# Block products in the last up stage of the first feed-forward network

## The chip, the cores and the metric

The kernel runs on one core of a Trainium2 chip. The metric is device time in microseconds (us) of one execution. The engines have their own instruction queues and run side by side: TensorE (PE in the profile, with its weight loads as PEld), VectorE (DVE), ScalarE (ACT), GpSimd (POOL) and SyncE (SP), which here only issues loads. POOL computes nothing in this kernel either; its queue carries a set of transfers from DRAM to DRAM.

## The reference, cut to what matters

Two layers, each a token mixer followed by a gated feed-forward network with a three-tap convolution between its two projections:

```python
def conv_ffn(h, up_w, conv_w, conv_b, down_w):
    u = dwconv(h @ up_w, conv_w, conv_b)
    a, v = jnp.split(u, 2, axis=-1)
    return (jax.nn.silu(a) * v) @ down_w

for i in range(DEPTH):                    # DEPTH = 2
    ...                                   # mixer: SSD scan (i = 0), differential attention (i = 1)
    xp = xp + p_g2 * conv_ffn(modulate(xp, norm_ffn_g[i], p_sh2, p_sc2), *ffn_p)
    xs = xs + s_g2 * conv_ffn(modulate(xs, norm_ffn_g[i], s_sh2, s_sc2), *ffn_p)
```

The model width is 1024, the hidden width 2816 (so the up projection has 2 × 2816 outputs). There are 640 tokens, 512 latent (xs) and 128 context (xp). All numbers are fp32.

## The kernel before, in words

**Matmuls.** Activations lie transposed, 128 features to a tile and 640 tokens along it. An fp32 number is held as a high part and a remainder, and each product is made of three matmuls: high × high, high × remainder, remainder × high. So each weight tile that arrives from DRAM (`raw`) is cast twice before use: ScalarE writes the high part `whi`, VectorE the remainder `wlo` (`split_w`). There are four `raw` buffers, and a load into one waits until VectorE has made the remainder of the tile that was in it. SP issues all these loads in one queue. `nextw` fetches the next weight tile in the order of a list (`weight_units`), loads some tiles ahead and casts `ahead` tiles ahead.

**The feed-forward network** (`ffn`, once per layer, l = 0 and 1). The hidden width makes 22 pairs of up tiles, one tile for the gate half `a`, one for the value half `v`. After each pair an epilogue runs: three convolution taps, SiLU, product, and the split into `mh` and `ml` (the high part and the remainder that the down projection reads). The pairs go in three groups (SUB); after each group, with one pair of lead, eight down tiles (`po`) add that group's share to the residual stream `xr`. For l = 0 the groups are pairs 0 to 7, 8 to 14 and 15 to 21, so that with the lead the last up stage makes pairs 16 to 21.

**A standard pair** is two up tiles of 8 × 3 × (256 + 384 columns): 96 matmuls for the pair.

**A pair by block products** (class `Blocks`). The two up tiles of a pair, the two halves of the 1024 inputs and the two halves of the 640 tokens form a 2 × 2 by 2 × 2 block product, which is made with seven products in place of eight. Each product is 4 × 3 matmuls of 320 columns, 84 for the pair. It needs sums of blocks on both sides:
- of activations, `T1`, `T2`, `T4` for each of four tiles, made once by `sums()`, and `T3`, which `finish_sums()` writes over parts of the activations themselves (`h01h`, `h01l` in the first network);
- of weights, four per pair, made in DRAM by transfers that add into their target (`weight_sums`, tile `wsum`, on POOL's queue, each transfer 768 KB for three pairs). They begin with small marks that make the queue wait for a certain `mh`, and they are later loaded like other weights, in two halves of 256 KB for one `raw` tile.

Products are accumulated in PSUM banks `ba`, `bb` and `bc`; between them ScalarE copies a bank (into `ua` or `uv`) and VectorE adds another bank to that copy. Products 3 and 4 of a pair are made while the next pair is under way (`third`, `fourth`); those of the last pair come within the first two down tiles (`between`).

Before the change the second network (l = 1) makes its pairs 5 to 21 this way (`STD = 5`), and the first network none.

**What else runs beside.** During the first network VectorE also computes the second layer's modulation (`mod_rest`, tiles `mw`, `cbc` and `junk`), as a task that advances at each `hook` between matmuls. A task can be finished at once with `drain`. The order of instructions on each engine is fixed when the program is built, by a scheduler; the tables of rows below show that order.

Of the kernel before, what the change touches and what calls it, by code (L numbers as in the profile page):

```python
# [41 lines left out]
STD = 5  # L42
# [8 lines left out]
class Blocks:  # L51
# [4 lines left out]
    def __init__(self, st, h, epilogue, pool):  # L56
        self.st, self.h, self.epilogue, self.pool = st, h, epilogue, pool
        self.pend = None
        self.spare = None
        self.half = None  # L60

    def sums(self):
# [3 lines left out]
        place = ["p"] * 5 + ["s"] + ["f"] * 6  # L66
        c1, c2 = slice(0, HT), slice(HT, T)
        for j in range(4):
# [17 lines left out]
            for i, x in ((1, t1), (2, t2), (4, t4)):  # L86
                pl, nm = place.pop(), f"T{i}_{j}"
                t = (st.slot("f", nm, F32R, bufs=NF) if pl == "f" else st.slot("sq", nm, F32R, bufs=1) if pl == "s"
                     else st.slot("T", nm, F32R, bufs=5, pool=self.pool))
# [81 lines left out]
class Step:  # L171
# [516 lines left out]
    def ffn(self, l, h, nextnorm, pool):  # L688
# [28 lines left out]
        blk = None  # L717
# [7 lines left out]
        for s, (k0, k1) in enumerate(sub):  # L725
# [3 lines left out]
            while done < end:  # L729
                if l and done >= STD:  # L730
                    blk.pair(done)
                else:
# [3 lines left out]
                    if l and done == STD - 1:  # L736
                        self.drain(sums)
                        blk.finish_sums()
                done += 1
            self.down = True  # L740
            if last and self.modtask:
                self.drain(self.modtask)
            if s == 1 - l:
                half = 3 * SUMS
                ends = range(STD, STD + half, SUMS) if l == 0 else range(STD + half, FT, SUMS)
                for p in ends:
                    self.weight_sums(p, min(p + SUMS, FT), mid[done - 2][0].bitcast(F32)[0:1, 0:2])
            if not last:
                self.project_out(mid, range(k0, k1), self.gate(l, 1), after=blk and blk.between)
            else:  # L750
                self.project_last(mid, range(k0, k1), self.gate(l, 1), nextnorm, parts="CD" if l else "AB",
                                  after=blk and blk.between)
# [550 lines left out]
    def weight_units(self):  # L1303
# [10 lines left out]
        def ffn(l):  # L1314
            both = lambda t: [(a["w_blk"][t].rearrange("h p n -> p h n"), wide)] if l else [(a["w_up"][t], wide)]
# [3 lines left out]
            def piece(i, p):  # L1319
                if i in (1, 2, 4):  # L1320
                    return a["w_blk"][p + FT * (i == 4), int(i > 1)], 512
                return (lambda: self.wsum[p - STD, (5, 6, 7, 3).index(i)]), 512

# [185 lines left out]
```

## Time and profile before

| | us |
|---|---|
| runs, median of 3 | 1874.46 (1874.0 to 1875.87) |
| profiled execution | 1877.01 |
| its span, first to last instruction | 1875.2 |
| TensorE busy | 1839.6 (98%) |
| VectorE busy | 1429.4 (76%) |
| ScalarE busy | 983.9 (52%) |
| mean granted TensorE clock | 0.991 |

The first network's stages in the trace: first up stage from 593, first down 699 to 755, second up 755 to 853.6, second down 853.6 to 903.4, last up 903.4 to 988.0, last down to about 1040. Attention fills 1040 to 1409, the second network the rest.

How to read it: the page is one execution. A row of the groups gives the line, engine, operation, out<-in with the program's tile names without their numbers, the shape, the count, then busy time and mean ns of one, then the idle time of the engine ahead of it and what ended it. In a timeline row the bracket at the end says how long the engine stood before it and for what; no bracket means that it did not stand. Lines are those of the kernel before: 220 is ScalarE's helper, 226 and 223 VectorE's, 229 the matmul, 252 the weight load and 1364 the weight sums.

### The profile page before, as it was taken

The numbers are of one execution on the slowest core, as the hardware profiler recorded it, in microseconds if no ns is written. First come the engines' busy times: TensorE is split into PE (matmuls) and PEld (weight loads), VectorE is DVE, ScalarE is ACT, GpSimd is POOL, SyncE is SP. The second block draws the span as 40 slices with busy tenths as digits, with TensorE's granted clock in tenths as the row PEclk, the third lists the DMA queues.
The fourth block names the chain that finished last, engine by engine and source line by source line (L and its number), as shares of the span: only waits on it lengthen the run. The fifth ranks groups of instructions, "written<-read, shape, count | busy, mean of one in ns | idle before, by whom it ended". The sixth has DMA issues, their size and how long they took to land.

```text
span 1875.2 us, 33004 instructions
## 1 busy us (share of the span) xinstructions
PE 1839.6 (98%) x13129; PEld 1727.2 (92%) x13129; DVE 1429.4 (76%) x2759; ACT 983.9 (52%) x1825; POOL 41.7 (2%) x64
## 2 busy tenths in 40 slices
PE   7999999999999999999999999999999999999997
PEld 4799899989989999999999988888899999999996
DVE  4689999999848999984454878778779874874864
ACT  2479686879426441342343566566546543643641
POOL 0000000000000000001110000000000011100000
PEclk9999999999999999999999999999999999999998
DMA  9734334346543656546773212111032268953421
GB/s 342 249 116 140 100 122 134 113 131 174 183 148 102 192 180 214 194 131 198 212 195 93 88 38 65 57 44 54 22 118 68 87 182 235 258 160 102 141 79 57
DMA packets 98386, 258.76 MB, mean 138 GB/s; under 512 B 11468, under 2 KB 18232, under 8 KB 93752
## 3 DMA queue, kind: packets, MB, share of 16 engines
q1 hardware_dynamic: 92152, 220.47, 36.3%
q0 software_dynamic: 5504, 35.66, 8.2%
q8 instruction: 103, 1.69, 0.4%
q10 hardware_dynamic: 576, 0.52, 0.1%
q14 instruction: 51, 0.42, 0.1%
HBM read 250.65 MB, written 41.61 MB: 156 GB/s over the span
## 4 chain that ended last, share of the span: by engine, by line
PE 93%; DVE 3%; ACT 2%; DMA 1%; issue 1%; SPq 0%; DVEq 0%; ACTq 0%
PE po L229 26%; PE up L229 18%; PE z L229 6%; PE x L229 5%; PE bc L229 5%; PE ba L229 5%; PE st L229 5%; PE bb L229 5%; PE v L229 3%; PE yp L229 3%; PE q L229 2%; PE sl L229 2%; PE k L229 2%; PE ov L229 2%; PE in L229 1%; PE wt L1237 1%
## 5 line engine op out<-in xcount | busy, mean ns | idle before, releaser
L220 ACT ACTIVATE whi<-raw 128x1024 fp32r<-128x1024 f32 (+4 forms) x257 | 261.9, 1020 | 363.9 <-PE po L229 226.1
L226 DVE TENSOR_TENSOR wlo<-raw,whi 128x1024 fp32r<-128x1024 f32 (+4 forms) x257 | 301.3, 1173 | 102.7 <-ACT whi L220 91.2
L223 DVE SCALAR_TENSOR_TENSOR xr<-po,mod,xr 128x256 f32<-128x256 f32 (+2 forms) x231 | 88.9, 433 | 148.7 <-PE po L229 148.6
L229 PE MATMUL po<-ml,whi 128*128 128x256 f32 (+1 forms) x704 | 168.4, 310 | 0.0
L229 PE MATMUL po<-mh,whi 128*128 128x256 f32 (+1 forms) x704 | 168.2, 311 | 0.0
L229 PE MATMUL po<-mh,wlo 128*128 128x256 f32 (+1 forms) x704 | 168.0, 310 | 0.0
L229 PE MATMUL up<-h01h,wlo 128*128 128x256 f32 (+1 forms) x656 | 149.4, 308 | 0.0
L229 PE MATMUL up<-h01h,whi 128*128 128x256 f32 (+1 forms) x656 | 149.3, 308 | 0.0
L229 PE MATMUL up<-h01l,whi 128*128 128x256 f32 (+1 forms) x656 | 149.3, 308 | 0.0
L229 PEld LDWEIGHTS po<-mh,whi 128*128 128x128 f32 x704 | 128.5, 188 | 0.5 <-ACT mh L220 0.2
L229 PEld LDWEIGHTS po<-ml,whi 128*128 128x128 f32 x704 | 128.8, 188 | 0.1
L229 PEld LDWEIGHTS po<-mh,wlo 128*128 128x128 f32 x704 | 128.9, 188 | 0.0
L229 PEld LDWEIGHTS up<-h01h,wlo 128*128 128x128 f32 x656 | 119.3, 188 | 0.0
L229 PEld LDWEIGHTS up<-h01h,whi 128*128 128x128 f32 x656 | 119.3, 188 | 0.0
L229 PEld LDWEIGHTS up<-h01l,whi 128*128 128x128 f32 x656 | 119.2, 188 | 0.0
L220 ACT ACTIVATE mh<-cv 128x640 fp32r<-128x640 f32 x44 | 32.4, 737 | 81.9 <-DVE cv L226 81.9
L220 ACT ACTIVATE e<-sl,sm 128x640 f32<-128x640 f32 x64 | 50.3, 789 | 39.5 <-DVE sm L1174 39.1
L229 PE MATMUL z<-h00h,whi 128*128 128x256 f32 (+1 forms) x256 | 62.9, 325 | 0.0
L220 ACT ACTIVATE ca<-ca 128x640 f32<-128x640 f32 x44 | 32.4, 736 | 58.0 <-DVE ca L223 58.0
L220 ACT ACTIVATE e<-rb,Ctok 128x128 f32<-128x128 f32 x160 | 56.3, 389 | 11.6 <-issue 9.2
L229 PE MATMUL z<-h00l,whi 128*128 128x256 f32 (+1 forms) x256 | 59.8, 311 | 0.0
L229 PE MATMUL z<-h00h,wlo 128*128 128x256 f32 (+1 forms) x256 | 59.7, 312 | 0.0
(557 smaller groups left out, 5025.4 us busy)
## 6 DMA issues: line engine op xcount, KB each, us to landing
mw<-in_modT SPq DMA_DIRECT2D x48, 512.0 KB, 3.3
wsum<-in_w_blk POOLq DMA_DIRECT2D x30, 768.0 KB, 7.0
raw<-in_w_up SPq DMA_DIRECT2D x44, 512.0 KB, 4.3
raw<-in_w_in SPq DMA_DIRECT2D x40, 512.0 KB, 5.3
rb<-rowd SPq DMA_DIRECT2D x40, 512.0 KB, 5.1
raw<-wsum SPq DMA_DIRECT2D x68, 256.0 KB, 2.9
raw<-in_w_dn SPq DMA_DIRECT2D x32, 448.0 KB, 3.4
raw<-in_w_qkv SPq DMA_DIRECT2D x24, 512.0 KB, 3.4
```

Source lines behind the costliest of these rows:

```text
L220: return self.nc.scalar.activation(out, in_, func, **k)
L223: return self.nc.vector.scalar_tensor_tensor(out, in0, s, in1, op0, op1)
L226: return self.nc.vector.tensor_tensor(out, a, b, op)
L229: return self.nc.tensor.matmul(out, lhsT, rhs, start=start, stop=stop, **k)
L1237: nc.tensor.transpose(pm[:, b * P:(b + 1) * P], ws[b][:, kc * P:(kc + 1) * P], self.ident)
```

## The change

Pairs 16 to 21 of the first network, which are its last up stage, are made by block products too (`STD = (16, 5)`, one number for each network). For this:

- The activation sums of the first network are made as a task during its second down stage, and finished (`drain`, `finish_sums`) at that stage's end. Their tiles lie in buffers that are free then: six in `f`, one in `sq`, two in `mw`, three in `cbc`. `mod_rest`, which uses `mw` and `cbc`, is therefore drained after pair 15 instead of ahead of the last down stage.
- The weight sums of these six pairs are two groups of eight transfers and two marks each, put on POOL's queue after pair 12, waiting for `mh` of pair 11. They stand ahead of the second network's first three groups.
- All up weights of the first network are now read from the block layout that the second network used (`w_blk`, now for both), whose rows are two runs of 512 numbers in place of one of 1024.
- The outer taps of pairs 16 to 21 are negated, as block products give these tiles with the other sign.

```diff
-STD = 5
+STD = (16, 5)
...
+        std = STD[l]
...
+        place = [lambda n: self.slot("f", n, F32R, bufs=NF)] * 6 + [lambda n: self.slot("sq", n, F32R, bufs=1)]
         if l:
-            blk = Blocks(self, h, epilogue, pool)
-            t = cw[:, FT + STD:, 0:3]
-            nc.vector.tensor_scalar(t, t, -1.0, None, ALU.mult)
+            place += [lambda n: self.slot("T", n, F32R, bufs=5, pool=pool)] * 5
+        else:
+            place += [lambda n: self.slot("mw", n, F32R, D, 2, pool)[:, :T]] * 2 + [spare(j) for j in range(3)]
+        blk = Blocks(self, h, epilogue, place)
+        t = cw[:, FT + std:, 0:3]
+        nc.vector.tensor_scalar(t, t, -1.0, None, ALU.mult)
...
-                if l and done >= STD:
+                if done >= std:
                     blk.pair(done)
...
+                if l == 0 and done == 13:
+                    for p in range(std, FT, SUMS):
+                        self.weight_sums(0, p, min(p + SUMS, FT), mid[done - 2][0].bitcast(F32)[0:1, 0:2])
...
             self.down = True
-            if last and self.modtask:
-                self.drain(self.modtask)
...
+            if l == 0 and done == std:
+                self.drain(self.modtask)
+                sums = self.add(blk.sums(), 1)
+            after = blk.between if blk.pend else None
...
+            if l == 0 and done == std:
+                self.drain(sums)
+                blk.finish_sums()
...
         def ffn(l):
-            both = lambda t: [(a["w_blk"][t].rearrange("h p n -> p h n"), wide)] if l else [(a["w_up"][t], wide)]
+            both = lambda t: [(a["w_blk"][l, t].rearrange("h p n -> p h n"), wide)]
...
-                return (lambda: self.wsum[p - STD, (5, 6, 7, 3).index(i)]), 512
+                return (lambda: self.wsum[l][p - STD[l], (5, 6, 7, 3).index(i)]), 512
```

In the rows that follow, a number behind a name of a weight tile is its place in the list of weights (tiles 97 to 104 are the second down stage's), that behind `ua`, `uv`, `ca`, `cv`, `mh`, `ml` the pair, and the number after the underscore only tells instances apart.

ScalarE around the start of the last up stage (pair 16), before:

```order
L220 ACTIVATE whi105_10017<-raw105_9891 128x1024
L220 ACTIVATE whi106_10078<-raw106_9953 128x1024
L220 ACTIVATE whi107_10140<-raw107_10015 128x1024
L220 ACTIVATE whi108_10216<-raw108_10076 128x1024
L220 ACTIVATE whi109_10277<-raw109_10138 128x1024
L220 ACTIVATE whi110_10353<-raw110_10214 128x1024
L220 ACTIVATE uraw_10135<-up_10075 128x640
L220 ACTIVATE ca_10195<-uraw_10135,fcw0_6711 128x640
L220 ACTIVATE ca_10195<-ca_10195 128x640
L220 ACTIVATE whi111_10412<-raw111_10275 128x1024
```

and in the changed kernel:

```order
L217 ACTIVATE whi106_10191<-raw106_10086 128x1024
L217 ACTIVATE whi107_10216<-raw107_10139 128x1024
L217 ACTIVATE ua16_10205<-ba_10203 128x320
L217 ACTIVATE whi110_10284<-raw110_10213 128x1024
L217 ACTIVATE ua16_10205<-ba_10203 128x320
L217 ACTIVATE whi111_10321<-raw111_10250 128x1024
L217 ACTIVATE uv16_10206<-ba_10203 128x320
L217 ACTIVATE ua17_10303<-bb_10204 128x320
L217 ACTIVATE whi108_10220<-raw108_10207 128x1024
L217 ACTIVATE whi109_10252<-raw109_10210 128x1024
L217 ACTIVATE whi112_10354<-raw112_10281 128x1024
L217 ACTIVATE whi113_10405<-raw113_10318 128x1024
```

The casts of tiles 105 to 110 stood in a row, ahead of the first copy out of PSUM. Now the casts of 110 and 111 stand between copies of pair 16, and those of 108 and 109 come after a copy of pair 17 (`ua17`).

SP, the loads of the same weight tiles, before:

```order
L252 DMA raw105_9891<-in_w_up 128x1024
L252 DMA raw106_9953<-in_w_up 128x1024
L252 DMA raw107_10015<-in_w_up 128x1024
L252 DMA raw108_10076<-in_w_up 128x1024
L252 DMA raw109_10138<-in_w_up 128x1024
L252 DMA raw110_10214<-in_w_up 128x1024
```

and in the changed kernel:

```order
L249 DMA raw105_10034<-in_w_blk 128x2x512
L249 DMA raw106_10086<-wsum0_72 128x512 x2
L249 DMA raw107_10139<-wsum0_72 128x512
L249 DMA raw107_10139<-in_w_blk 128x512
L249 DMA raw108_10207<-in_w_blk 128x512
L249 DMA raw109_10210<-wsum0_72 128x512
L249 DMA raw109_10210<-in_w_blk 128x512
L249 DMA raw110_10213<-wsum0_72 128x512 x2
L249 DMA raw111_10250<-in_w_blk 128x2x512
L249 DMA raw112_10281<-wsum0_72 128x512
L249 DMA raw108_10207<-wsum0_72 128x512
L249 DMA raw112_10281<-wsum0_72 128x512
```

Each tile was one load of 1024 columns, in order. Now most consist of two halves, one of them or both from the sums, and the second half of tile 108 is issued behind the first half of tile 112.

VectorE, the remainder of weight tile 116, before (there it is the second tile of pair 21):

```order
L223 SCALAR_TENSOR_TENSOR cv_10473<-uraw_10465,fcw0_6711,cv_10473 128x511
L223 SCALAR_TENSOR_TENSOR cv_10473<-uraw_10465,fcw0_6711,cv_10473 128x127
L226 TENSOR_TENSOR cv_10473<-ca_10467,cv_10473 128x640
L226 TENSOR_TENSOR ml18_10482<-cv_10473,mh18_10481 128x640
L226 TENSOR_TENSOR wlo116_10755<-raw116_10620,whi116_10754 128x1024
L223 SCALAR_TENSOR_TENSOR ca_10601<-uraw_10542,fcw0_6711,ca_10601 128x511
L223 SCALAR_TENSOR_TENSOR ca_10601<-uraw_10542,fcw0_6711,ca_10601 128x127
```

and in the changed kernel (there it holds the weights of product 6 of pair 19 and of product 4 of pair 18):

```order
L223 TENSOR_TENSOR cv_10530<-ca_10524,cv_10530 128x640
L223 TENSOR_TENSOR uv18_10438<-uv18_10438,bb_10436 128x320
L223 TENSOR_TENSOR ml17_10539<-cv_10530,mh17_10538 128x640
L223 TENSOR_TENSOR ua19_10576<-ua19_10576,bc_10575 128x320
L223 TENSOR_TENSOR ua18_10437<-ua18_10437,bb_10436 128x320
L223 TENSOR_TENSOR wlo116_10508<-raw116_10439,whi116_10507 128x1024
L220 SCALAR_TENSOR_TENSOR ca_10657<-ua18_10437,fcw0_6712,ca_10657 128x511
L223 TENSOR_TENSOR wlo117_10558<-raw117_10472,whi117_10557 128x1024
L220 SCALAR_TENSOR_TENSOR ca_10657<-ua18_10437,fcw0_6712,ca_10657 128x511
```

Before, `wlo116` stood between the end of one pair's epilogue and the convolution of the next; now it stands directly behind an addition of a PSUM bank to `ua18`.

POOL's queue, first rows with transfers, before:

```order
L1367 DMA wsum_72<-mh14_9412 2x1x1 x5
L1364 DMA wsum_72<-in_w_blk 32x3x2048 x4
L1364 DMA wsum_72<-wsum_72 32x3x2048
L1364 DMA wsum_72<-in_w_blk 32x3x2048 x3
L1364 DMA wsum_72<-wsum_72 32x3x2048
L1364 DMA wsum_72<-in_w_blk 32x3x2048 x3
L1364 DMA wsum_72<-wsum_72 32x3x2048
L1367 DMA wsum_72<-mh14_9412 2x1x1
```

and in the changed kernel (`wsum0` belongs to the first network, `wsum1` to the second):

```order
L1385 DMA wsum0_72<-mh11_8999 2x1x1 x4
L1382 DMA wsum0_72<-in_w_blk 32x3x2048 x4
L1382 DMA wsum0_72<-wsum0_72 32x3x2048
L1382 DMA wsum0_72<-in_w_blk 32x3x2048 x3
L1382 DMA wsum0_72<-wsum0_72 32x3x2048
L1382 DMA wsum0_72<-in_w_blk 32x3x2048 x3
L1382 DMA wsum0_72<-wsum0_72 32x3x2048
L1385 DMA wsum1_73<-mh14_9434 2x1x1 x4
L1382 DMA wsum0_72<-in_w_blk 32x3x2048
L1382 DMA wsum1_73<-in_w_blk 32x3x2048
L1382 DMA wsum0_72<-wsum0_72 32x3x2048
L1382 DMA wsum1_73<-in_w_blk 32x3x2048
```

The queue began with the second network's sums, waiting for `mh14`. Now it begins with those of the first, waiting for `mh11`, and the second network's follow, partly mixed in.

More of the change, by code (lines that the diff above doesn't have):

```diff
@@ L1327, in ffn @@
                 end = min(k1 + 1, FT)
-                while done < end and not (l and done >= STD):
+                while done < min(end, STD[l]):
                     out += up(done)
@@ L1378, in run @@
         tc, nc, a = self.tc, self.nc, self.a
-        self.wsum = self.dram.tile([FT - STD, 4, P, 512], F32, tag="wsum", name="wsum")
+        self.wsum = [self.dram.tile([FT - STD[l], 4, P, 512], F32, tag=f"wsum{l}", name=f"wsum{l}") for l in range(2)]
         self.units = self.weight_units()
```

46 lines of the change are left out of this document (24 added, 22 removed).

## The prediction

> **What bounds the kernel now.** I read the page first, then busy times by stage, then the matmuls one by one where one stage ends and the next begins.
>
> ```profile
> PE 1839.6 (98%) x13129; PEld 1727.2 (92%) x13129; DVE 1429.4 (76%) x2759; ACT 983.9 (52%) x1825; POOL 41.7 (2%) x64
> PE 93%; DVE 3%; ACT 2%; DMA 1%; issue 1%; SPq 0%; DVEq 0%; ACTq 0%
> 790.00:818.00 28.00, 28.00 (x193) 28.00 (x192) 27.97 (x49) 13.02 (x16) 0.00 (x0) 1.00 0.54 174
> 818.00:848.00 30.00, 30.00 (x206) 30.00 (x206) 22.43 (x39) 15.07 (x19) 2.13 (x4) 1.00 0.27 81
> 855.00:900.00 45.00, 45.00 (x305) 45.00 (x305) 19.58 (x35) 8.86 (x10) 5.90 (x8) 1.00 0.77 213
> 900.00:990.00 90.00, 90.00 (x615) 90.00 (x614) 45.85 (x70) 39.18 (x48) 11.07 (x15) 1.00 0.78 198
> 1570.00:1656.00 86.00, 85.41 (x566) 82.78 (x565) 64.63 (x102) 50.75 (x73) 11.78 (x16) 1.00 0.88 241
> ```
>
> The columns of the stage rows are the stretch, its length, busy PE, PEld, DVE, ACT and POOL with counts, the granted clock, the DMA share and GB/s. TensorE is the bound: 98% of the span, 93% of the chain that ended last, and not a hundredth of a microsecond idle in the first network's stages, at a full granted clock. The second network, which already uses block products, does idle (85.41 of 86.00). So what the change removes from PE comes off the span one to one, and each wait it puts before a matmul goes on again.
>
> **The edit that saves: six pairs by seven products.**
>
> ```profile
> 903.44 0.46 PE L229 MATMUL up<-h01h,whi 128*128 128x256 f32 x2
> 903.73 0.46 PE L229 MATMUL up<-h01l,whi 128*128 128x256 f32 x2
> 987.97 0.45 PE L229 MATMUL po<-mh,whi 128*128 128x256 f32 x2
> 1485.23 0.31 PE L229 MATMUL ba<-h11h,wlo 128*128 128x320 f32 x1
> 1485.38 0.31 PE L229 MATMUL ba<-h11h,whi 128*128 128x320 f32 x1
> ```
>
> The last up stage runs from 903.44 to 987.97: 84.53 us for six pairs. A pair of matmuls (256 and 384 columns) takes 903.73 − 903.44 = 0.29 us; one block matmul of 320 columns takes 1485.38 − 1485.23 = 0.15. That is the same time per column, so the work follows the count: 84 of 320 columns in place of 96 (48 × 640/320). 84.53 × 12/96 = **10.57 us saved**. The two products that hang over (3 and 4 of pair 21) move into the first two down tiles and are in this count.
>
> [...]
>
> **What it costs: casts.** A standard tile needs one 1024-column cast (high half on ACT, remainder on DVE) for 48 matmuls; a block pair reads 3584 columns where a standard pair reads 2048, in less time. ACT has 39.18 of 90 us in that stage and DVE 45.85, so the sum fits, as it does in the second network (50.75 and 64.63 of 86). What matters is the order of the casts.
>
> ```profile
> L220 ACT ACTIVATE whi<-raw 128x1024 fp32r<-128x1024 f32 x30 | 31.7, 1058 | 54.1 <-PE po L229 26.0 <-PE bb L229 14.4 <-PE ba L229 11.2
> L226 DVE TENSOR_TENSOR wlo<-raw,whi 128x1024 fp32r<-128x1024 f32 x30 | 36.6, 1221 | 16.5 <-ACT whi L220 16.5
> L220 ACT ACTIVATE ua<-ba 128x320 f32<-128x320 f32 x12 | 5.1, 425 | 4.5 <-PE ba L229 4.5
> L226 DVE TENSOR_TENSOR ua<-ua,ba 128x320 f32<-128x320 f32 x6 | 2.9, 487 | 4.4 <-PE ba L229 4.4
> L229 PE MATMUL ba<-h11h,whi 128*128 128x320 f32 x71 | 22.7, 320 | 0.0
> 1493.67 0.56 PE L229 MATMUL ba<-T,whi 128*128 128x320 f32 x2 [0.53 <-ACT uv L220]
> 1636.69 0.41 PE L229 MATMUL bb<-h11h,whi 128*128 128x320 f32 x1 [0.59 <-ACT ua L220]
> PE bb L229 <- ACT ua L220: 1.3, 3, 0.6
> PE ba L229 <- ACT uv L220: 0.5, 1, 0.5
> ```
>
> Reading: a cast is 1.06 us on ACT and then 1.22 on DVE; a PSUM copy 0.42 on ACT, an add 0.49 on DVE; a matmul ends some 0.31 us after it begins, 0.16 after the next could begin. Where a copy must follow the very matmul before the waiting one, PE stood 0.53 to 0.59 us. All four waits of the second network's 17 pairs are of that kind, 1.8 us together; no cast is late there. In the changed order of the first network three casts stand late. I count matmuls from the first of pair 16.
>
> (a) Matmul 72, the first of product 2 of pair 17: ACT does the copy ua17, which needs matmul 71, and only then whi108, the tile of this product. PE stands 0.16 + 0.42 + 1.06 = 1.65 us with the handovers. After four matmuls (0.59) it needs wlo108, 1.25 behind whi108: another 0.66. Together **2.3**. Queued behind whi108 on ACT are whi109, whi112 and the first convolution of pair 16; those have over 20 matmuls of slack.
>
> (b) Matmul 264, the first of product 6 of pair 19: DVE's add ua18 needs matmul 263, 0.16 + 0.49 + handovers = 0.70, and wlo116 stands right behind it on DVE: 1.22 − 0.59 = 0.65. **1.35**.
>
> (c) Matmul 324 waits for the copy ua20 of matmul 323: **0.6**, like the quoted rows. Matmul 338 then waits for the add ua20 of 335 (0.4) and 340 for wlo119 behind it (0.9): **1.3**.
>
> (d) Seven further waits have 3 to 5 matmuls of slack (0.44 to 0.73 us) against a copy with handovers of 0.8 less what the last matmul overlaps. I take 0.2 for one with 3, and 0.4 for the one at matmul 101, where two adds on DVE follow the same matmul: **0.6**. Ends: 0, and 7 × 0.59 = 4.
>
> **Loads on SP.** The second half of raw108 is issued behind the first half of raw112, which waits for wlo110, whose whi110 stands behind the copy ua16. That is matmul 28 at 4.1 us, the add to 4.9, the cast to 6.1 after the stage's start. ACT wants raw108 at matmul 72 plus the copy, 11.2 us.
>
> ```profile
> raw<-wsum SPq DMA_DIRECT2D x28, 256.0 KB, 5.9
> raw<-in_w_blk SPq DMA_DIRECT2D x4, 512.0 KB, 5.4
> wsum<-in_w_blk POOLq DMA_DIRECT2D x18, 768.0 KB, 6.9
> raw<-in_w_up SPq DMA_DIRECT2D x12, 512.0 KB, 4.5
> ```
>
> The median landing of 256 KB beside the POOL queue's transfers is 5.9 us (the first two rows are of 1516 to 1656, the others of 840 to 990), so the half lands at 12.1: **0.9** more in (a). Ends 0 and 4, a landing near 9. The other loads of this network come from the block layout with shorter runs, 5.4 against 4.5 us; a tile has 7 us of PE time and loads run three tiles ahead, so they cost nothing; with that cover gone each would cost that 0.9.
>
> **The weight sums on POOL's queue.** Sixteen more transfers of 768 KB are made, from mh11 on.
>
> ```profile
> 805.97 0.74 ACT L220 ACTIVATE mh<-cv 128x640 fp32r<-128x640 f32 x1 [0.69 <-DVE cv L226]
> 845.87 2.77 POOL L1367 DMA_DIRECT2D wsum<-mh  x5 [845.42 <-ACT mh L220]
> 848.63 0.59 POOL L1364 DMA_DIRECT2D wsum<-in_w_blk  x1
> 864.62 0.90 POOL L1364 DMA_DIRECT2D wsum<-in_w_blk  x1 [6.88 <-issue]
> 874.21 0.59 POOL L1364 DMA_DIRECT2D wsum<-wsum  x1 [8.70 <-issue]
> 983.74 0.87 POOL L1364 DMA_DIRECT2D wsum<-in_w_blk  x1 [3.84 <-DMA wsum<-wsum]
> 1523.70 0.58 POOL L1364 DMA_DIRECT2D wsum<-in_w_blk  x1 [0.34 <-issue]
> 1654.64 0.84 POOL L1364 DMA_DIRECT2D wsum<-in_w_blk  x1 [4.74 <-DMA wsum<-wsum]
> ```
>
> Before, 24 such transfers are issued from 848.63 to 983.74: 5.87 us each. From mh11's end at 806.7, with small marks as before, the first goes at 810.5. The sum that raw106 reads, the seventh transfer, lands at 810.5 + 6 × 5.9 + 7 = 853; SP reaches raw106 only when wlo102 frees its buffer, about 879. The one for raw116 (the fourteenth) lands at 894 against 920. The last, for raw119 (two transfers of the second network's sums are mixed in, so the eighteenth), lands at 917; matmul 336 wants it at 903.4 + 49.4 + 5 = 958, less 7 for load and cast. At the traced pace all are in time: **0**. The second network's 24 then end near 1046 instead of 990, and are first read after 1482. DMA engines have room: 0.27 busy at 818 to 848, plus what these transfers added after (0.77 at 855 to 900).
>
> **The activation sums in the second down stage.**
>
> ```profile
> 854.53 1.09 DVE L226 TENSOR_TENSOR wlo<-raw,whi 128x896 fp32r<-128x896 f32 x1 [3.56 <-ACT whi L220]
> 866.29 1.13 DVE L223 SCALAR_TENSOR_TENSOR xr<-po,mod,xr 128x256 f32<-128x256 f32 x3 [3.74 <-PE po L229]
> 867.34 1.08 DVE L226 TENSOR_TENSOR wlo<-raw,whi 128x896 fp32r<-128x896 f32 x1
> 825.02 1.21 DVE L668 CUSTOM_DVE_ANT_0 junk<-mw,cbc 128x1024 bf16<-128x1024 f32 x1
> ```
>
> Four rounds of two 640-column adds, four 320-column sums and three remainders cost DVE 4 × (2 × 0.8 + 7 × 0.48) = 20 us, and 2 more for the rewritten halves; ACT 16 copies of 0.42, 7 us. DVE has 25.4 of 45 us free there. All rounds but the last come before wlo102: adding them up from wlo101 at 854.5, wlo102 ends near 879, and PE wants it at matmul −122, 885.5. Covered: **0**; with DVE 7 us later it would be a stall. The modulation that is drained earlier was done at 826, before that place: 0. Negating the taps is one small instruction in each network: 0.
>
> **Sum.** −10.57 + 2.3 + 0.9 + 1.35 + 0.6 + 1.3 + 0.6 = **−3.5 us**. Against the profiled span of 1875.2 that is 1871.7; that run took 1877.01 with what lies around it, and the median of the runs is 1874.46, so the median should be **1871.0**. A difference of 0.2% (3.75 us) is about what a measurement of this kernel tells from no change; the forecast lies almost on that bound.
>
> **Rivals.**
> 1. *The stalls don't come.* If casts and loads are only as late as in the second network, 1.8 us in 17 pairs becomes 0.7 in six: gain 9.9, 1864.6. For it: that network shows no late cast. Against: there at least 49 matmuls lie between a cast's last dependence and its use, here 0, 4 and 4. Chance 0.15.
> 2. *The weight sums come late, slower than before.* raw119 needs an average of under (951 − 7 − 810.5)/17 = 7.85 us per transfer; above it PE stands at matmul 336, with SP's queue behind it. At 8.7 us the eighteenth lands at 965, 14 us late: 1885. For it: one gap before was 874.21 − 864.62 = 9.6, and POOL's transfers now start while DVE is at 27.97 of 28 us. Against: in the second network, where DVE is 75% busy (64.63 of 86), 24 transfers from 1523.70 to 1654.64 take 5.7 us each, no longer than beside a DVE at 19.58 of 45. Chance 0.10. [...]
> 3. *The pinches are longer.* (d) at its upper end 4 and raw108 at 4: stalls of 13 instead of 7, 1877.5; a small loss. Chance 0.12.
> 4. *The change doesn't do what it says*: the saving is there but attention, whose loads and first casts are re-ordered, gives back 3 us: 1874. Its stages idled a few us in all before. Within the bound; chance 0.10.
>
> **How the numbers follow.** The forecast's own case, 1868 to 1873.5, has 0.53: some 0.30 of it below 1870.7 and 0.23 above. Faster: 0.30 + 0.15 = 0.45. Same: 0.23 + 0.10 + 0.03 of rival 3 = 0.36. Slower: 0.10 + 0.09 = 0.19. The range runs from rival 1 to rival 3, 1864.5 to 1878, and leaves out rival 2 and a little at each end.
>
> **What would show it.** The distance from the first block matmul to the first whole down tile; PE idle of 2 to 3.5 us named ACT whi, DVE wlo or a load some 10.6 us into the stage, about 1.4 at DVE ua or wlo near 42 us, and about 2 near 52 us; none in the down stage before it. POOL's issues should go from 810 on at 5.9 us. I would be wrong if PE waits there for raw<-wsum, if the three pinches are absent, or if the block matmuls step at other than 0.147 us.

## The result, and the profile after

The change made the kernel slower: 1883.95 us (median of 6 runs, 1882.19 to 1887.19) against 1874.1 (1872.26 to 1875.87) on the same chip, a ratio of 1.0056 [1.0044, 1.0069]. The forecast was 1871.0. The profiled execution took 1887.19 us with a span of 1885.4, 10.2 longer than the span before; it is the slowest of the six runs.

The page of the changed kernel, busy time by engine and the chain that ended last:

```profile
PE 1836.9 (97%) x13057; PEld 1719.3 (91%) x13057; DVE 1465.6 (78%) x2827; ACT 999.6 (53%) x1862; POOL 55.6 (3%) x84
...
PE 89%; DVE 4%; DMA 3%; ACT 2%; issue 1%; SPq 0%; DVEq 0%; ACTq 0%
```

PE has 72 matmuls fewer but only 2.7 us less busy time, and its share of the chain fell from 93% to 89%: it now waits. The waits of PE between 903 and 1110 us, from the first block product to the first scores of attention (engine, line, for whom; us in total, times, longest):

```profile
PE sl L226 <- ACT e L217: 2.8, 3, 1.6
PE ba L226 <- ACT uv L217: 2.7, 1, 2.7
PE bc L226 <- ACT whi L217: 1.8, 1, 1.8
PE q L226 <- ACT v L217: 1.6, 1, 1.6
PE bc L226 <- DVE wlo L223: 1.1, 2, 0.7
...
```

Before, PE waited only twice from 903 to 1110 us, 0.2 us at 1046.7 and 0.6 us at 1086.7. PE's timeline of the changed kernel has its waits one by one; the first row begins the block products, at the same time as the standard ones before (903.44):

```profile
903.38 0.30 PE L226 MATMUL ba<-h01h,whi 128*128 128x320 f32 x1
...
914.12 0.42 PE L226 MATMUL bb<-h01h,whi 128*128 128x320 f32 x1 [1.05 <-DVE uv L223]
917.94 0.41 PE L226 MATMUL bc<-h01h,whi 128*128 128x320 f32 x1 [1.79 <-ACT whi L217]
919.20 0.63 PE L226 MATMUL bc<-h01h,wlo 128*128 128x320 f32 x1 [0.41 <-DVE wlo L223]
919.63 0.47 PE L226 MATMUL bc<-h01h,whi 128*128 128x320 f32 x1
919.90 0.47 PE L226 MATMUL bc<-h01l,whi 128*128 128x320 f32 x1
...
922.76 0.31 PE L226 MATMUL bb<-h01h,whi 128*128 128x320 f32 x1
922.91 0.31 PE L226 MATMUL bb<-h01l,whi 128*128 128x320 f32 x1
...
949.99 0.53 PE L226 MATMUL bb<-T,whi 128*128 128x320 f32 x2 [0.67 <-DVE ua L223]
951.03 0.42 PE L226 MATMUL bb<-T,wlo 128*128 128x320 f32 x1 [0.23 <-DVE wlo L223]
960.03 0.42 PE L226 MATMUL ba<-h01h,whi 128*128 128x320 f32 x1 [0.53 <-ACT ua L217]
962.71 0.56 PE L226 MATMUL ba<-T,whi 128*128 128x320 f32 x2 [0.36 <-DVE ua L223]
963.94 0.41 PE L226 MATMUL bc<-h01h,wlo 128*128 128x320 f32 x1 [0.66 <-DVE wlo L223]
976.84 0.82 PE L226 MATMUL ba<-T,whi 128*128 128x320 f32 x2 [2.68 <-ACT uv L217]
```

The nine waits in brackets add up to 8.38 us. Behind the first three, matmuls step 919.90 − 919.63 = 0.27 us, not the 0.15 of 922.91 − 922.76. The stage rows show why: the granted clock (third last column).

```profile
919.00:923.00 4.00, 3.80 (x16) 3.80 (x17) 2.90 (x4) 0.78 (x1) 0.00 (x0) 0.58 0.96 206
923.00:975.00 52.00, 48.63 (x318) 46.31 (x316) 38.60 (x60) 29.38 (x41) 5.84 (x8) 1.00 0.86 243
975.00:979.00 4.00, 2.16 (x8) 2.16 (x9) 2.18 (x4) 2.01 (x3) 0.87 (x1) 0.74 1.00 340
979.00:983.00 4.00, 4.00 (x22) 3.73 (x22) 1.95 (x4) 1.83 (x3) 0.00 (x0) 0.83 1.01 224
```

After the first waits, and again after the single one of 2.68, the clock is lower for some 3 us. In shorter stretches the trace has 1.00 from 918.5 to 918.9 and 0.50 from 919.2 to 922.0, so the clock had already fallen when the third wait ended. Adding up, over all starts in the stage, by how much each step exceeds 0.147 (0.293 for a pair) gives 7.26 us, about 3 of it in these two slow stretches; most of the rest is at matmuls that wait for a copy, an add or a cast, and at the one behind each of them: these step 0.1 to 0.16 us longer, even where little or no idle time is recorded.

No trace here gives a rule for what makes the clock fall: here it fell after waits of 1.05 and 1.79 us, and after one of 2.68 (0.50 from 977.0 to 980.0); in e5 (below), behind waits of 1.05, 2.34 and 0.40 us at the same matmuls, the steps are 0.15 us again from the second matmul on, and not 0.27.

From the first block product to the last down matmul (1044.3 us) it is 140.9 us; before it was 136.0 (903.44 to 1039.4). So the change lost 4.9 there: −10.57, +8.38 and +7.26 make +5.1. From there to the first score matmul (`sl`) it is 40.2 us (1084.5), before 34.3: another 5.9.

### The profile page after: what moved, and what is told of

Same layout as the page of the kernel before. It is cut to its first block, busy times and chain, and to the rows that moved or that the text cites. A ratio compares the mean times of both kernels' runs of the same rounds, so it can differ in the third digit from the quotient of the medians.

```text
span 1885.4 us, 33063 instructions
## 1 busy us (share of the span) xinstructions
PE 1836.9 (97%) x13057; PEld 1719.3 (91%) x13057; DVE 1465.6 (78%) x2827; ACT 999.6 (53%) x1862; POOL 55.6 (3%) x84
## 4 chain that ended last, share of the span: by engine, by line
PE 89%; DVE 4%; DMA 3%; ACT 2%; issue 1%; SPq 0%; DVEq 0%; ACTq 0%
PE po L226 24%; PE up L226 13%; PE bb L226 6%; PE z L226 6%; PE ba L226 6%; PE x L226 5%; PE bc L226 5%; PE st L226 5%; PE v L226 3%; PE yp L226 3%; PE sl L226 2%; PE k L226 2%; PE q L226 2%; PE ov L226 2%; PE in L226 1%; PE wt L1255 1%
## 5 line engine op out<-in xcount | busy, mean ns | idle before, releaser
L217 ACT ACTIVATE whi<-raw 128x1024 fp32r<-128x1024 f32 (+4 forms) x266 | 270.4, 1020 | 326.6 <-PE po L226 199.2
L223 DVE TENSOR_TENSOR wlo<-raw,whi 128x1024 fp32r<-128x1024 f32 (+4 forms) x266 | 312.4, 1177 | 78.7 <-ACT whi L217 67.8
L226 PEld LDWEIGHTS po<-mh,whi 128*128 128x128 f32 x704 | 128.0, 188 | 1.0 <-ACT mh L217 0.8
L226 PE MATMUL up<-h01h,whi 128*128 128x256 f32 x464 | 105.6, 308 | 0.0
L226 PE MATMUL up<-h01h,wlo 128*128 128x256 f32 x464 | 105.6, 308 | 0.0
L226 PE MATMUL up<-h01l,whi 128*128 128x256 f32 x464 | 105.6, 308 | 0.0
L226 PEld LDWEIGHTS up<-h01h,whi 128*128 128x128 f32 x464 | 84.4, 188 | 0.0
L226 PEld LDWEIGHTS up<-h01l,whi 128*128 128x128 f32 x464 | 84.4, 188 | 0.0
L226 PEld LDWEIGHTS up<-h01h,wlo 128*128 128x128 f32 x464 | 84.4, 188 | 0.0
L226 PE MATMUL bb<-T,whi 128*128 128x320 f32 x264 | 61.4, 312 | 0.7 <-DVE ua L223 0.7
L665 DVE CUSTOM_DVE_ANT_0 junk<-mw,cbc 128x1024 bf16<-128x1024 f32 x48 | 58.6, 1221 | 3.5 <-DMA mw<-in_modT 3.5
```

The lines of the kernel that those rows point to most:

```text
L217: return self.nc.scalar.activation(out, in_, func, **k)
L223: return self.nc.vector.tensor_tensor(out, a, b, op)
L226: return self.nc.tensor.matmul(out, lhsT, rhs, start=start, stop=stop, **k)
L665: nc.vector.tensor_tensor_reduce(w if c else junk, w, cb[:, c, :], 1.0, 0.0, ALU.mult, ALU.add, self.mod[l][:, t, c:c + 1])
```

## The experiments

Three theories stood at the start, and all are about what the forecast costed at nothing or small. *Order*: the scheduler lists the casts and the loads as if the sums came late, and PE waits for what stands late in the list. *Crowding*: the sixteen transfers on POOL's queue take DMA time from loads at a place where something is short. *Attention*: the rope table's load, which now stands behind ten weight loads in SP's order and not six, delays attention. All edits are to the changed kernel unless said otherwise; medians with the range, the ratio to the kernel before in the same session with its 95% interval.

| run | median us (range, runs) | before | ratio |
|---|---|---|---|
| e1 sums after pair 8 | 1879.38 (1874.75–1882.63, 10) | 1874.13 | 1.0024 [1.0013, 1.0035] |
| e2 the same, rope early | 1879.17 (1874.67–1881.66, 6) | 1874.13 | 1.0028 [1.0016, 1.0039] |
| e3 second network's sums moved | 1907.49 (1905.38–1911.84, 4) | 1874.13 | 1.0186 [1.0171, 1.0201] |
| e4 before, rope late | 1875.14 (1872.07–1876.7, 11) | 1874.13 | 1.0006 [0.9997, 1.0015] |
| e5 changed, rope early | 1884.37 (1881.53–1889.52, 6) | 1874.23 | 1.0063 [1.0049, 1.0077] |
| e6 e5, sums after pair 11 | 1874.28 (1868.98–1881.38, 12) | 1874.23 | 1.0000 [0.9989, 1.0012] |
| e7 e5, sums after pair 10 | 1872.89 (1869.03–1877.36, 12) | 1874.23 | 0.9991 [0.9981, 1.0000] |
| e8 no sums for the first network | 1867.68 (1866.96–1869.91, 5) | 1874.23 | 0.9968 [0.9956, 0.9980] |
| e9 sums in the mixer | 1867.79 (1862.39–1870.95, 7) | 1873.4 | 0.9959 [0.9945, 0.9974] |
| e10 e9, transfers repeated, unread | 1872.06 (1867.59–1877.08, 11) | 1873.4 | 0.9994 [0.9983, 1.0004] |
| e11 changed again | 1883.11 (1879.54–1886.52, 6) | 1873.4 | 1.0048 [1.0033, 1.0063] |

**e1, the sums early.**

```diff
-                if l == 0 and done == 13:
+                if l == 0 and done == 9:
```

> The changed kernel with one edit: the first network's weight sums go on POOL's queue after pair 8 (waiting for mh7) instead of after pair 12. In the order that the scheduler then writes, the casts of tiles 108, 116 and 119 stand in front of the copies that they stood behind. Theory A (late casts in the order): the waits of 1.05, 1.8+0.4, 0.7+0.2 and 0.5+0.4+0.7 us in the last up stage shrink to at most 2 us in all, the two stretches of slow clock go, and the last down stage ends 6 us or more sooner than in the changed kernel (from 1044.3 to 1038 or less); the rope table stays behind eight loads of the query, key and value weights, so attention's start still loses some 5 us; total 1875 to 1878. Theory B (transfers crowd each other): the sums of the second network still run through the stage, loads still land after 6 us, and at least 5 us of waits stay; total 1881 or more.

The block stage was mended: one wait of 0.4 us is left, and from the first block product to the last down matmul it is 128.2 us. But the transfers now ran beside the modulation loads of the second up stage, and the first block product begins at 917.1, 13.7 us later than in the changed kernel. The total, 1879.4, lies between the two theories, each of which has a part. The stage's row, before and then in e1:

```profile
699.00:800.00 101.00, 101.00 (x690) 101.00 (x690) 99.21 (x177) 29.98 (x35) 0.00 (x0) 1.00 0.63 200
```

```profile
699.00:800.00 101.00, 93.37 (x621) 92.14 (x619) 76.40 (x135) 16.72 (x20) 9.73 (x13) 0.98 0.92 272
```

e1's issues in that stage (count, KB each, median us to landing), and its waits of PE and of DVE from 690 to 860 us:

```profile
mw<-in_modT SPq DMA_DIRECT2D x20, 512.0 KB, 7.1
wsum<-in_w_blk POOLq DMA_DIRECT2D x9, 768.0 KB, 9.6
```

```profile
PE up L226 <- ACT uraw L217: 5.8, 2, 4.8
PE up L226 <- DVE xr L220: 4.0, 2, 3.0
```

```profile
DVE junk L665 <- DMA mw<-in_modT: 24.8, 10, 3.6
```

DVE had 1.8 us to spare there before (99.21 of 101). The modulation loads land in 7.1 us and not 3.3, DVE waits 24.8 us for them, and PE waits 9.8 for DVE's and ACT's work behind that. So crowding is real, and of the places tried for these sums it cost most here, where DVE is full and fed by loads.

**e2 and e4, the rope table.** e2 is e1 with the first attention weight tile (number 134) cast outside the first network's pool, so that attention's small loads come earlier; e4 does the reverse to the kernel before (tile 125 cast inside the pool).

```diff
-            wp, t, b = (self.pw, "w", 3) if self.px is None or u % 5 < 3 else (self.px, "x", 2)
+            wp, t, b = (self.pw, "w", 3) if self.px is None or u % 5 < 3 or u == 134 else (self.px, "x", 2)
```

```diff
-            wp, t, b = (self.pw, "w", 3) if self.px is None or u % 5 < 3 else (self.px, "x", 2)
+            wp, t, b = (self.pw, "w", 3) if self.px is None or u % 5 < 3 and u != 125 else (self.px, "x", 2)
```

> As the run before, and the cast of weight tile 134 (the first tile of attention's projections) is put in the buffers that outlive the first network, instead of in the network's own pool; in the order the rope table's load then stands behind five weight loads, not eight. Theory A': the rope table waits for the network's memory, which tile 134 holds until attention's first tiles are done; with the tile elsewhere the load is issued near 1035 to 1045, PE reaches the first score matmul about 10 us after the first q matmul as before (it took 14 in the changed kernel), and 4 to 6 us come off against the run with the early sums alone: 1869 to 1873. Rival: attention starts late because of the POOL transfers that run until 1060; then nothing moves against that run.

> The kernel before with one edit: the cast of the first tile of attention's projections (125 there) is put in the first network's pool, as its number happens to do in the changed kernel. The up and down stages keep their order, the rope table's load moves from behind six weight loads to behind eight. Theory A': the load is issued near 1066 instead of 1039.8 and the kernel is 4 to 6 us slower, 1878 to 1880, all of it between 1040 and 1110. Rival (order of these loads does not matter, the crowded transfers do): no difference from before within 1 us.

In e2 the rope load went out at 1045.0 and not 1065.7 (e1), with no effect on the time (1869 to 1873 was expected, so the rival held); e1's stretch into attention was no longer than before. e2 loses in the second up stage as e1 does (PE waits 9.0 us from 690 to 860), though its lists on ACT, DVE and SP are row for row those of e10 (below), which has no wait of PE there; so that loss is made by the transfers, not by the order. In e4 it went out at 1061.5 and not 1039.8; the stretch grew from 34.3 to 35.9 us and the time by 0.06%, within what can be told. So a rope load some 20 us later, behind eight weight loads, is worth at most 1 to 2 us. The changed kernel has ten ahead of it, which e4 doesn't test.

**e3, the second network's sums moved into attention.**

```diff
-                for p in ends:
-                    self.weight_sums(1, p, min(p + SUMS, FT), mid[done - 2][0].bitcast(F32)[0:1, 0:2])
+        for p in range(STD[1], FT, SUMS):
+            self.weight_sums(1, p, min(p + SUMS, FT), self.cv[0:1, 0:2])
```

> The changed kernel with all weight sums of the second network made during attention (waiting for the table cv), so that the last up stage has only the end of the first network's own sums beside it; the casts of the last up stage stay in the changed kernel's order. Theory A: loads land in 3 to 4 us after the first 15 us, the wait of 2.7 us at the copy uv20 (ACT held by a cast whose down weights had not come) goes with the slow clock behind it, but the waits at matmuls 60, 72, 264, 324 and 338 stay, 5 to 6 us; the last down stage ends 4 to 5 us sooner; the rope table is still late, behind eight loads; total 1878 to 1880. Theory B: all waits of the stage vanish, 1872 or less.

The largest waits in the block stage:

```profile
PE bc L226 <- ACT whi L217: 1.5, 1, 1.5
PE bc L226 <- DVE wlo L223: 1.1, 2, 0.7
PE bb L226 <- DVE uv L223: 1.0, 1, 1.0
PE bb L226 <- DVE ua L223: 0.7, 1, 0.7
PE ba L226 <- ACT ua L217: 0.5, 1, 0.5
```

The block stage kept its pinches (5.4 us; the wait of 2.68 is gone), which therefore don't come from these transfers. That was theory A, but its total, 1878 to 1880, was missed by some 28 us, because attention lost far more. One kind of its small transfers between 1060 and 1300 us (in the kernel before it landed in 1.5 us), and its largest wait of PE, which the kernel before doesn't have:

```profile
out_kout<-kp SPq DMA_DIRECT2D x7, 64.0 KB, 5.8
```

```profile
PE wt L1250 <- ACT wpT L217: 11.2, 4, 3.5
```

**e5, e6 and e7, the sums one step at a time.** e5 is the changed kernel with e2's line and with all marks of a group of sums issued ahead of its transfers; e6 and e7 then start the first network's sums one and two pairs earlier.

```diff
-                    for p in range(std, FT, SUMS):
-                        self.weight_sums(0, p, min(p + SUMS, FT), mid[done - 2][0].bitcast(F32)[0:1, 0:2])
+                    ps = range(std, FT, SUMS)
+                    self.weight_marks(0, ps, mid[done - 2][0].bitcast(F32)[0:1, 0:2])
+                    for p in ps:
+                        self.weight_sums(0, p, min(p + SUMS, FT))
```

```diff
-                if l == 0 and done == 13:
+                if l == 0 and done == 12:
```

> The changed kernel with its sums at their old place and two edits that touch attention's start alone: the cast of weight tile 134 goes to the buffers that outlive the first network, and all marks of a set of weight sums are issued ahead of its transfers, so that no mark that reads the first network's mh stands late in POOL's queue. In the order the rope table's load then stands behind five weight loads, not ten. Theory: the 5.7 us that the changed kernel lost between its last down tile and its first score matmul come back (34 us for that stretch, not 40), the last up stage keeps its 5 to 8 us of waits; total 1877 to 1879. Rival (attention's start is slow because POOL's transfers run until 1060): the stretch stays at 40 us and the total at 1883.

> As the run before, and the first network's weight sums start one pair sooner, after pair 11 (waiting for mh10, about 792). In the order the casts of tiles 108 and 116 then stand in time; only the waits near matmuls 324 to 340 are left. Theory (late casts): the stage's waits fall from 8.4 us to 2 to 3 with no slow clock, the last down stage ends near 1034 to 1036, total 1866 to 1871. Rival (crowding): the transfers overlap the modulation's loads from 792 to 816, the second up stage loses what the last one gains; total 1874 or more.

> As the run before, one pair sooner still (after pair 10, waiting for mh9, about 777). Theory: the order of the last up stage is about the same as with pair 11, so its waits are too (2 to 3 us), and the only difference is the overlap with the modulation's loads until 816: 40 us instead of 24. If crowding grows with the overlap, the second up stage loses 1 to 4 us and the kernel is that much slower than with pair 11; with a start after pair 8 (110 us of overlap) it lost some 14 us.

e5 issued the rope load at 1042.5; in its trace, which is of its fastest execution, the stretch into attention is 36.4 us and not 40.2. The median didn't follow: it is as slow as the changed kernel, so this theory failed by its own number. One pair earlier (e6) is worth 10 us at once. The waits in the block stage, the four largest of e5 and then the three largest of e6:

```profile
PE bc L226 <- ACT whi L217: 2.3, 1, 2.3
PE ba L226 <- ACT uv L217: 1.7, 1, 1.7
PE bb L226 <- DVE uv L223: 1.2, 2, 1.1
PE bc L226 <- DVE wlo L223: 1.1, 2, 0.7
```

```profile
PE ba L226 <- DVE ua L223: 0.7, 1, 0.7
PE bc L226 <- DVE wlo L223: 0.6, 1, 0.6
PE ba L226 <- ACT ua L217: 0.5, 1, 0.5
```

As many transfers run in e6; the list of casts is another, and the largest waits are gone. e6's traced execution (1870.77) is in the range of its theory, but its median, 1874.28, is the rival's, though the second up stage loses nothing in the trace (the first block product is at 902.4). e7 has one wait of 2.3 us for `uv` again; that it is faster than e6, and not slower as expected, is within what can be told.

**e8, no sums for the first network.**

```diff
-                if l == 0 and done == 13:
-                    for p in range(std, FT, SUMS):
-                        self.weight_sums(0, p, min(p + SUMS, FT), mid[done - 2][0].bitcast(F32)[0:1, 0:2])
...
+                if l == 0:
+                    return a["w_blk"][l, p + FT * (i == 7), int(i == 6)], 512
```

> As the runs before, and no weight sums are made for the first network: products that need one read a plain block of the same weight in its place, loaded in the same two halves, so these six pairs' results are left out of what the kernel computes. All other work stays. This is what the block products are worth alone. Theory: 10.6 us saved, about 2.5 lost to short waits and restarts in the stage, none in the second up stage: total 1865 to 1867. If loads or casts still make PE stand for over 3 us here, the sums were not the cause of it.

So the block products by themselves, with their casts well placed and without their own sixteen transfers, are worth 6.5 us in the medians (1874.23 − 1867.68), not 10.57. The stage with its down tiles takes 128.0 us against 136.0.

**e9, the sums in the mixer.** e5 with the same sums issued some 310 us earlier (the lines after pair 12 go), where the mixer's output projection leaves the DMA engines free (from 495 to 620 us their share was 0.38; with the sums it is 0.78, and PE has no wait there). The lists of PE, ACT and DVE are e8's, row for row.

```diff
         hy = [self.split(xf[2 + i // 4][i % 4], f"y{8 + i}") for i in range(8)]
+        ps = range(STD[0], FT, SUMS)
+        self.weight_marks(0, ps, hy[0][0].bitcast(F32)[0:1, 0:2])
+        for p in ps:
+            self.weight_sums(0, p, min(p + SUMS, FT))
```

> The kernel of the rope experiment (tile 134 and the marks moved), and the first network's weight sums are made some 300 us sooner, beside the end of the mixer (waiting for y8, about 495), ahead of the modulation's loads. In the order all casts of the last up stage then stand in time, as without sums. Theory: what the changed kernel lost is the place of these transfers, by the order they bring and by the loads they crowd; here both are gone, so the total is that of the kernel without sums, 1866 to 1869, with under 1 us of waits in the last up stage and none in the second. Rival: the transfers cost what they cost wherever they run; then PE waits in the mixer between 500 and 600 and the total is 1872 or more.

It beats both kernels: 0.9959. The six pairs' block products pay when their weight sums are made out of the way. The last up stage itself is no emptier than in the changed kernel, since the second network's transfers now run there (DMA share 0.89 from 905 to 985 us, against 0.86). Nor is the mixer's place always free: in the trace of e10, which has the same program there, ACT waits 4.1 us for a load and PE then 2.2 us, near 550.

**e10 and e11, the crowd without the order.** e10 is e9 with the sixteen transfers made a second time, after pair 12, into a table that nobody reads; nothing on PE, ACT, DVE or SP is listed otherwise than in e9. e11 is the changed kernel again.

```diff
+                if l == 0 and done == 13:
+                    ps = range(std, FT, SUMS)
+                    self.weight_marks(2, ps, mid[done - 2][0].bitcast(F32)[0:1, 0:2])
+                    for p in ps:
+                        self.weight_sums(2, p, min(p + SUMS, FT))
```

> As the run before, and the same sixteen transfers are made a second time, after pair 12 as in the changed kernel, into a table that nobody reads. The order of every other engine is that of the run before, so this adds crowding alone, with the second network's sums pushed back as in the changed kernel. Theory A (order): with casts in time, late landings are covered; within 1.5 us of the run before. Theory B (crowding): loads land after 6 us and more, ACT and PE wait for some of them in the last up stage and the last down stage, differently in each execution: 4 to 8 us slower than the run before, and a spread of runs of 6 us or more where the run before has 3. What is left up to the 1884 of the rope experiment is then the order's.

> The changed kernel itself once more, beside the two runs before, for a second trace and more times. If the loss between the last down tile and the first score matmul is made by the place of the rope table's load in SP's queue, the stretch is 40 us in this trace too; if it comes from the state of POOL's transfers it can be anything from 34 to 40. The waits that the order makes (near matmuls 60, 72, 264, 324, 338) must be the same within 0.3 us; the one at the copy uv20, made by a late load, need not be. Total 1882 to 1886.

The transfers run in e10 as they do in the changed kernel: these are the issues from 905 to 1045 us, of the changed kernel and then of e10 (count, KB each, median us to landing).

```profile
wsum<-in_w_blk POOLq DMA_DIRECT2D x16, 768.0 KB, 7.9
raw<-wsum SPq DMA_DIRECT2D x18, 256.0 KB, 6.2
...
raw<-in_w_dn SPq DMA_DIRECT2D x8, 448.0 KB, 6.0
```

```profile
wsum<-in_w_blk POOLq DMA_DIRECT2D x16, 768.0 KB, 7.5
raw<-wsum SPq DMA_DIRECT2D x15, 256.0 KB, 5.3
...
raw<-in_w_dn SPq DMA_DIRECT2D x8, 448.0 KB, 7.2
```

The down weights land even later in e10. Yet from its first block product (902.30) to its last down matmul (1030.5) it takes 128.2 us, as e9 does, and the changed kernel 140.9, e11 141.1. That difference of 12.7 us goes with the order: idle 8.38 against 0.45, longer steps 7.26 against 2.49. ACT's timeline shows it at matmul 72, the changed kernel and then e10:

```profile
916.18 0.44 ACT L217 ACTIVATE ua<-bb 128x320 f32<-128x320 f32 x1 [2.64 <-PE bb L226]
916.83 2.95 ACT L217 ACTIVATE whi<-raw 128x1024 fp32r<-128x1024 f32 x3 [0.21 <-DMA raw<-wsum]
```

```profile
915.02 1.06 ACT L217 ACTIVATE whi<-raw 128x1024 fp32r<-128x1024 f32 x1 [2.54 <-PE bb L226]
915.98 0.42 ACT L217 ACTIVATE ua<-bb 128x320 f32<-128x320 f32 x1
```

In e10 the cast `whi` stands ahead of the copy `ua17`, in the changed kernel behind it. e11's waits at the five places named are those of the first trace within 0.35 us (within 0.01 but for matmul 72, where 1.47 stands against 1.79), and its stretch into attention is 40.3; only the wait for `uv` is 1.69 with 0.71 before it, where it was 2.68. So these belong to the program, not to one execution.

The reverse, the changed kernel's order without the crowd, is nearly what e3 has. Its lists on ACT, DVE and SP are the changed kernel's row for row until behind this stage, and its last transfer on POOL's queue is issued at 904.7, as the stage begins; from 905 to 985 us the halves from the sums land in 2.9 us, against 6.2, and the DMA share is 0.47, against 0.86. The waits at matmuls 60, 264, 268, 324, 338 and 340 are there all the same, to 0.01 us; that at 72 is 1.47, and the one for `uv` is gone. The stage with its down tiles takes 136.2 us. So, one trace each, 8.0 us of the 12.7 stay with the order when the crowd is gone (136.2 − 128.2), and the other 4.7 take both. No run has the casts in time and no crowd; but with the casts in time 0.45 us of idle is all that the crowd could have made.

In the medians the ladder is: e9 1867.8; the sixteen transfers at the old place again (e10) +4.3; the changed kernel +11.0 more. Where e10 loses its 4.3 its trace doesn't show; that trace is of one of its faster executions (1869.8). The scatter doesn't tell either: e10's runs are 9.5 us apart, and e9's 8.6.

## Why the prediction was wrong

The forecast put the median 3.5 us lower; the span came out 10.2 us longer, 13.7 apart. The idle time in the sum, 7.05 us, came near: 8.38 was measured, 1.3 more. The step that failed is what the sum put at nothing: each wait was charged its idle time alone, and the matmuls behind the waits cost another 7.26 us; and attention, left out of the sum, cost 5.9. (What is left, 0.8 the other way, lies in the down tiles and behind the first scores.)

**The saving** (−10.57). The block matmul steps 0.15 us, as forecast. (The two rows quoted there can't show that a step goes by its columns alone, as a pair of 256 and 384 columns is two matmuls too; single steps before, from 1019.8 to 1028.2 us, can: 0.118 us for 256 columns and 0.175 for 384, near the ratio of the columns.) But a product with waits of its own isn't bare matmul time: even in e9 and e10, with the casts well placed, 0.45 us of idle and 2.49 of longer steps go back, and the stretch gains 7.8 (136.0 to 128.2). This term was too large by some 3 us. The second network would have told: its 17 pairs of before have 1.9 us of idle and, added up in the same way, some 6 of longer steps, which makes 2.8 for six pairs. I took from them the waits alone.

**The pinches** (a), (b) and (c) were right in place, and as a whole too large. (a) 2.3 and 0.9: 1.79 + 0.41 = 2.2 (e11: 1.9), of which 0.21 is the load. (b) 1.35: 0.67 + 0.23 = 0.9. (c) 0.6 and 1.3: 0.53, and 0.36 + 0.66 = 1.0. Together 4.65 against 6.45. That e3 has them without the crowd beside them shows that they come from the order, as the prediction had it.

**Small waits** (d), 0.6 with ends of 0 and 4, was the term for idle time that was mis-sized most: the waits not in (a) to (c) are 1.05 and 2.68, 3.7 us in all, near the upper end. That the idle time as a whole came near is luck, 3.1 too little here against 1.8 too much above. One wait is at matmul 60, which the prediction doesn't name: DVE's add `uv16` stands behind ACT's copy `uv16`, so that two steps and not one must fit into the slack. The other is a chain. ACT holds a down cast ahead of the copy `uv20`, and that cast's weights were late; ACT's timeline:

```profile
975.51 0.95 ACT L217 ACTIVATE whi<-raw 128x896 fp32r<-128x896 f32 x1 [2.86 <-DMA raw<-in_w_dn]
976.37 0.42 ACT L217 ACTIVATE uv<-ba 128x320 f32<-128x320 f32 x1
```

I had costed the other loads at 0 because they run three tiles ahead. The down weights land in 6.0 us here where they took 4.2 before, and what stood behind them on ACT was a copy with a few matmuls of slack. This one needs both, the order and the crowd: it is gone in e3 and in e10.

**What follows a wait** was not in the sum at all: of the 7.26 us, the lower clock is about 3, some 2.5 are there even with the casts in time, and the rest is longer steps behind the late casts.

**The weight sums** at 0 held for the sums themselves: the first transfer went at 811.19 (forecast 810.5), the next 28 at 6.2 us each (forecast 5.9), and from 860 to 1040 us ACT waits 1.0 us in all for loads of sums, PE for none itself. "DMA engines have room" did not hold: the DMA share is 0.86 from 923 to 975 us, the down weights land 1.8 us later, and the sixteen transfers cost +4.3 in the medians even with the casts in time (e10).

**Attention** was rival 4, at 3 us and a chance of 0.10. It is 5.9 us in the trace, and 6.0 in e11's. The rope table's load goes out at 1071.4, not 1039.8, and DVE waits for it; PE then waits at the first scores (DVE's and PE's timelines):

```profile
1077.64 0.69 DVE L223 TENSOR_TENSOR ru<-ru,rope 128x512 f32<-128x512 f32 x1 [2.47 <-DMA rope<-in_rope]
```

```profile
1084.50 0.56 PE L226 MATMUL sl<-kh,qh 64*128 64x320 f32 x2 [1.61 <-ACT e L217]
```

With ten weight loads ahead of it, that load goes out 27.1 us after the last down matmul (27.0 in e11); with eight, in e1, e3 and e4, 20.4 to 21.1 us after it, and there the stretch is 34.3, 34.4 and 35.9. In e9, e10 and e5, with five, it goes out at 1030.7, 1030.9 and 1042.5, and the stretch is 35.5, 36.6 and 36.4. So only the place behind ten loads goes with 40. No run has that place without the transfers beside it, so whether slow landings are needed too is open; and e5, which mends the place, does not lower the median.

Rival 2 has the right time, 1885, for a wrong reason: the transfers took 6.2 us each and not 8.7, and no sum came late. From the first to the fifth (811.19 to 834.79) they are 5.9 us apart with DVE busy 20.62 of 23.60 us, so that a busy DVE holds them up was not shown. Rival 3, longer pinches, is the nearest in the stage, and rival 4 in attention; neither has a cost behind the waits.

## What to carry to other kernels

Transfers that "have room" are to be placed, not only counted: the same sixteen, 310 us earlier, turned 0.5% slower into 0.4% faster, and where DVE lives on loads (e1) they cost 13.7 us, more than the change could gain. When a scheduler orders the work by when it believes data to arrive, moving the data early also mends the order of casts that nobody touched; so compare the order of a copy and a cast at each place with little slack, and follow the chain through two engines, not one. Sum the recorded waits, then add what stands behind them: longer first steps, and the clock (here 7.26 us beside 8.38 of waits).

## What the runs showed of the hardware

In the changed kernel TensorE's granted clock fell from 1.00 to 0.50 at 918.9 us, after waits of 1.05 and 1.79 us, and again at 977.0, after one of 2.68, and was back some 3 us later each time; behind waits of 1.05, 2.34 and 0.40 us at the same matmuls of e5 the steps show no fall (0.15 us, not 0.27). In the changed kernel a matmul that waited, and the one behind it, stepped 0.1 to 0.16 us longer, beside the wait itself (0.26 us from 960.03 to 960.29, then 0.15). In e1, from 699 to 800 us, the loads of 512 KB beside transfers of 768 KB from memory to memory on POOL's queue landed in 7.1 us, against 3.3 in the kernel before, which has no such transfers there; the transfers took 9.6 to land.
